# The order of the loads on one queue: an expert stage's weights against the memory weights and rows that follow them

## The chip, the cores and the metric

The kernel runs on one core of one Trainium2 chip. The metric is the time of one execution on the device in microseconds, as the median of several runs. All times in the rows are microseconds from the start of the profiled span, unless they are marked ns.

## What is computed

The reference is one hybrid transformer block (two attentions, then 32 experts of which each of 512 tokens uses two), followed by a second block of two layers, A and B, each of which also attends to 256 memory rows. All of it is float32. The change touches the experts and the step from them to layer A:

```python
for e in range(N_EXPERTS):                                   # 32, EXPERT_FF = 256
    hid = jax.nn.silu(jnp.matmul(h, w_gate[e])) * jnp.matmul(h, w_up[e])
    out = out + jnp.matmul(hid, w_down[e]) * combine[:, e:e + 1]
...
x = rmsnorm(x + m, final_norm_g)                             # the first block's end
...
kv = rms_norm(mem, mem_gain) @ w_kv                          # for layer A and for layer B
h = rms_norm(x, norm_gain[l])
cols = h @ w_in
```

## The kernel before

A matrix product in full precision is made from three products of split operands: each weight unit of 128 x 1024 floats (512 KB) is loaded raw, copied into a high part on ACT (line 229) and subtracted into a low part on DVE, every eighth on POOL (line 232). The experts' units are used raw, without a split.

All weights go through one object, `Stream` (line 196 on), in the order of one plan. `advance` emits loads (lines 214 and 217, all on SP's queue) in the plan's order as far as `ahead` allows, and stops at the first unit whose ring of tiles is full; `get` calls `advance` and hands out the next unit. A plan entry names its lane, that is, the ring that it is loaded into. The experts' 192 units are spread over seven lanes, so that tiles that are free in this stage serve as weight tiles: m (12 tiles), x (4), h (3), p and q (5 each: the high and low parts of the split weights), v (3: the raw weights), t (4). `_dealt` deals them out: the first 19 units are twelve m, four x and three h, then all lanes mix, and the last 32 units use m, x and h, the last 16 only m and h. The units of a pair of experts are 8 for gate and up and 4 for down; the first 8 units are pair 0's gate and up, then each step brings the next pair's 8 and this pair's 4. After the experts' units stand layer B's memory weights: four w_mv and four w_mk, in lane w.

The loop over the pairs (lines 1468 to 1493) is a block in which PE, ACT, DVE and POOL keep the order of the program: gate and up of the next pair (`gate_up`, line 1405), turning the tokens that `gather` fetched (`turn_tokens`, line 1390), the turned hidden row (`turned`, line 1418), and down (`down`, line 1431), whose result POOL scatters into `yd` (line 1436). SP isn't in that block: a scheduler places SP's instructions by its own estimate of when they can run, within what their tiles allow.

At j = 13 the loop emits the loads of the memory rows for layer B, two halves in tiles of ring m (`mem_load`, line 634), and reads the number of further rounds of experts into a register of each engine (line 1492). At j = 14 `ws.upto` lets the first two of w_mv be split. Behind the loop `mem_split` splits the memory halves, and `upto` lets all eight memory weights be split as far as tiles allow. Then the rows of x1, the residual, are loaded back (line 1501), and each engine reads a branch over the further rounds (an If, line 1549), which isn't taken here.

Behind the If, SP loads the row of gains gF (line 1077) and the experts' results from `yd` (lines 1563 and 1564), DVE adds them to x1's rows (lines 1566 and 1567), PE makes layer B's memory rows meanwhile (lines 370 to 372), turns x2 (line 404) and goes on with layer A. R (line 428), the rows' norms, needs the square of gF.

Of the kernel before, what the change touches and what calls it, by code (L numbers as in the profile page):

```python
# [16 lines left out]
AF = mybir.ActivationFunctionType  # L17
# [292 lines left out]
def build(tc, A, out, dbg=None):  # L310
    nc = tc.nc
    ctx = ExitStack()
    dbg = dbg or {}
    V, S, G, T = nc.vector, nc.scalar, nc.gpsimd, nc.tensor
# [8 lines left out]
    def acc():  # L323
        return ps.tile([128, 512], F32, name="acc", tag="acc", bufs=2)
# [191 lines left out]
    def pump(steps, n=None):  # L516

        if n != 0:
            for i, _ in enumerate(steps):
                if i + 1 == n:  # L520
                    return

    def xtile(name):
        return xp.tile([128, 1024], F32, name=name, tag="xn", bufs=4)
# [45 lines left out]
    ws = Stream(nc, [(ap, "w") for ap in plan1 + kv0] + moe_u + [(ap, "w") for ap in plan2], ahead=3)  # L570
# [58 lines left out]
    def mem_load(pool):  # L629

        res = []
        for j in range(2):
            res.append(pool.tile([128, 1024], F32, name="mem", tag="mraw", bufs=MR))
            nc.sync.dma_start(res[j], mTd[:, 1024 * j:1024 * j + 1024])
        return res

    def mem_split(pool, raw):
        res = []
        for t in raw:
            hi, lo = (pool.tile([128, 1024], F32R, name="mT", tag="mT", bufs=4) for _ in range(2))  # L640
            S.activation(hi, t, AF.Copy)
            V.tensor_tensor(lo, t, hi.bitcast(F32), OP.subtract)
            res += [(hi[:, q:q + 256], lo[:, q:q + 256]) for q in range(0, 1024, 256)]
        return res
# [429 lines left out]
    def bcast_row(pool, off, n, name, tag=None, bufs=1):  # L1074
        t = pool.tile([128, n], F32, name=name, tag=tag or name, bufs=bufs)
        r = A["rows"]
        nc.sync.dma_start(t, bass.AP(tensor=r.tensor, offset=r.offset + off, ap=[[0, 128], [1, n]]))
        return t
# [53 lines left out]
    x1v = x1d.rearrange("(c p) d -> c p d", p=128)  # L1132
# [57 lines left out]
    order = ExitStack()  # L1190
# [186 lines left out]
    def gather(j, ix):  # L1377

        nc.gpsimd.indirect_dma_start(out=xgs[j % 2], out_offset=None, in_=x1d,
                                     in_offset=bass.IndirectOffsetOnAxis(ap=ix, axis=0),  # L1380
                                     bounds_check=511, oob_is_err=False)

    def turn_tokens(j):

        xg = xgs[j % 2]
        res = []
        for q in range(2):
            tp = tpp()
            for k in range(4):
                T.transpose(tp[:, k * 128:k * 128 + 128], xg[:, (4 * q + k) * 128:(4 * q + k) * 128 + 128], ident)  # L1390
            t = hchunk("xgt")
            V.tensor_tensor(t.rearrange("p (k n) -> p k n", k=4), tp.rearrange("p (k n) -> p k n", k=4),  # L1392
                            vec(V_FFN + 4 * q, 4)[:, :, None].to_broadcast([128, 4, 128]), OP.mult)
            res += [t[:, k * 128:k * 128 + 128] for k in range(4)]
        return res
# [3 lines left out]
    def gate_up(get, X, p, us):  # L1399

        for u in us:
            w = [get(), get()]
            for k in range(2):
                for e, z in enumerate(sides):
                    T.matmul(p[z], X[2 * u + k][:, z], w[e][k], start=u + k == 0, stop=u + k == 4)  # L1405

    def hidden(p, hr, w):

        th = hchunk("th")[:, :256]
        S.activation(th, p[:, :256], AF.Tanh, scale=hr)  # L1410
        V.scalar_tensor_tensor(th, th, 1.0, p[:, :256], op0=OP.add, op1=OP.mult)
        V.scalar_tensor_tensor(th, th, w, p[:, 256:], op0=OP.mult, op1=OP.mult)
        return th

    def turned(th):
        tp = tpp()
        for k in range(2):
            T.transpose(tp[:, k * 128:k * 128 + 128], th[:, k * 128:k * 128 + 128], ident)  # L1418
        t = hchunk("hid")[:, :256]
        S.activation(t, tp[:, :256], AF.Copy)  # L1420
        return t

    def down(get, t, ox):

        y = big("y", "y", 2)
        for n in range(2):
            w = [get(), get()]
            p = scp()
            for k in range(2):
                for e, z in enumerate(sides):  # L1430
                    T.matmul(p[z], t[:, k * 128 + NS * e:k * 128 + NS * e + NS], w[e][k], start=k == 0, stop=k == 1)  # L1431
            if n:
                V.tensor_copy(y[:, 512:], p)  # L1433
            else:
                S.activation(y[:, :512], p, AF.Copy)
        nc.gpsimd.indirect_dma_start(out=yd, out_offset=bass.IndirectOffsetOnAxis(ap=ox, axis=0),
                                     in_=y, in_offset=None, bounds_check=1023, oob_is_err=False)
# [23 lines left out]

    order = ExitStack()
    ET = mybir.EngineType
    order.enter_context(tc.manual_schedule(engines={ET.PE, ET.Activation, ET.DVE, ET.Pool}))
    own = len(plan1) + 8 + 192
    ws.upto = own
    pg, Xnext = acc(), None
    for j in range(-1, 16):
        if j >= 0:
            th = hidden(pg, rw[:, j:j + 1], cw[:, j:j + 1])  # L1470
        if j < 15:
            Xg = Xnext or Xg
            pg = acc() if j >= 0 else pg
            gate_up(ws.get, Xg, pg, range(3))
        if j < 14:
            Xnext = turn_tokens(j + 2)
            if j < 12:
                gather(j + 4, idx[:, j + 4:j + 5])
        if j >= 0:
            t = turned(th)  # L1480
        if j < 15:
            gate_up(ws.get, Xg, pg, range(3, 4))
        if j >= 0:
            down(ws.get, t, odx[:, j:j + 1])
        if j == 0:
            pump(kv)
        if j == 13:
            mem2 = mem_load(mo)
        if j == 14:
            ws.upto = own + 2  # L1490
        if j == 13 and not dbg.get("noif"):
            nv = nc.values_load(next_i[0:1, 0:1], min_val=0, max_val=14)
    mT = mem_split(mo, mem2)
    ws.upto = own + 8
    ws.advance()
    order.close()
    vB_steps = memory_steps(ws, mT, store_v, (scp, otp))

    x2 = [xtile("x2") for _ in range(4)]
    for c in range(4):  # L1500
        nc.sync.dma_start(x2[c], x1v[c])


    def extra(e):
# [47 lines left out]
    gF = bcast_row(mo, 0, 1024, "gF", "mraw", MR)  # L1552
# [3 lines left out]
    ms = []  # L1556
    gF2 = big("gF2", "mraw", MR)
    with tc.manual_schedule(engines={ET.PE, ET.Activation, ET.DVE, ET.Pool}):
        S.activation(gF2, gF, AF.Square)
        kmB = [mo.tile([128, 512], F32, name="kmB", tag="mraw", bufs=MR) for _ in range(2)]  # L1560
        ms, ms2 = ([big("m", "mraw", MR) for c in range(4)] for _ in range(2))
        for c in range(4):
            nc.sync.dma_start(ms[c], yd[128 * c:128 * c + 128, :])
            nc.sync.dma_start(ms2[c], yd[512 + 128 * c:640 + 128 * c, :])
        def add_experts(c):
            V.tensor_tensor(x2[c], x2[c], ms[c], OP.add)
            V.tensor_tensor(x2[c], x2[c], ms2[c], OP.add)
            tap("x2", x2[c], c)

        def square(c):  # L1570
            S.activation(ms[c], x2[c], AF.Square, accum_out=s3[:, c:c + 1])
        pump(vB_steps, AFTER[0])
        add_experts(0)
        pump(vB_steps, AFTER[1])
        add_experts(1)
        square(0)
        pump(vB_steps)
        kv = mem_k(1, mT, mo, lambda j: kmB[j])
        tps = [bank() for bank in (scp, scp, scp, otp, tpp, tpp)]

        def beside(c):
            if c != 1:
                pump(kv, AFTER[c + 2])
            if c in (0, 2):
                add_experts(2 + c // 2)
            if c == 3:
                ws.upto = own + 10
                ws.advance()
        hT = transposed(x2, gFA, hp_, "h", 16, tps=tps, more=scp, before=beside)
        ws.upto = None  # L1590
        for c in range(1, 4):
            square(c)
        for c in range(4):
            V.tensor_tensor_reduce(ms2[c], ms[c], gF2, 1.0, 0.0, OP.mult, OP.add, s4[:, c:c + 1])

        V.tensor_scalar(a12[:, 1], s3, 1.0 / 1024, EPS, OP.mult, OP.add)
        V.tensor_scalar(a12[:, 0], s4, 1.0 / 1024, None, OP.mult)
        V.scalar_tensor_tensor(a12[:, 0], a12[:, 1], EPS, a12[:, 0], op0=OP.mult, op1=OP.add)
        G.tensor_tensor(r12, a12, mhalf.rearrange("p (a c) -> p a c", a=2), OP.pow)
        pump(kv, 2)  # L1600
# [493 lines left out]
```

## Time and profile before

| | us |
|---|---|
| median of 3 runs | 1861.84 |
| lowest and highest | 1859.59 and 1862.24 |
| the profiled execution | 1861.34 |
| its span | 1859.6 |
| PE busy | 1797.6 (97%) |
| DVE, ACT, POOL busy | 881.7, 731.5, 359.4 |
| queue of SP | 77184 packets, 248.43 MB |

The page of the profile gives busy times for the whole span and then in 40 slices of 46.5 us; the experts lie in slices 11 to 16. Busy shares of the span are a mean over stages with different limits, so the stage is to be read from views of its own stretch.

### The profile page before, as it was taken

How to read it: one execution, taken by the hardware profiler on the slowest of the kernel's cores; microseconds unless marked ns; L12 is line 12 of the kernel's file. 1: busy time of each engine (PE TensorE's matmuls, PEld its weight loads, DVE VectorE, ACT ScalarE, POOL GpSimd, SP SyncE). 2: the span in 40 equal slices, each digit the busy share in tenths (PEclk: the TensorE clock that was granted, in tenths of full speed). 3: DMA queues.
4: the chain of work that ended last, by engine and by line, in shares of the span. 5: the costliest groups of instructions: out<-in, count | busy, mean ns of one | idle time of the engine just before them, and what ended most of it. 6: DMA issues, size and time to landing. Idle time of an engine off the chain costs nothing.

```text
span 1859.6 us, 25386 instructions
## 1 busy us (share of the span) xinstructions
PE 1797.6 (97%) x9466; PEld 1386.2 (75%) x9466; DVE 881.7 (47%) x1864; ACT 731.5 (39%) x1747; POOL 359.4 (19%) x461
## 2 busy tenths in 40 slices
PE   8999999999899886999999999999999999999999
PEld 8857776788533322798989799989788787777887
DVE  4389765365422112842443422342575336667571
ACT  5475355343101002534554424454563333233450
POOL 1301200011211101114424104524200002212210
PEclk9999999999999998999999999999999999999999
DMA  5221222178999998532311122311242332211231
GB/s 180 79 69 35 74 69 74 57 247 302 354 413 410 405 407 333 223 127 91 104 56 53 62 91 91 100 59 46 69 135 93 114 106 65 68 58 58 69 113 57
DMA packets 82787, 261.14 MB, mean 140 GB/s; under 512 B 11872, under 2 KB 13792, under 8 KB 82656
## 3 DMA queue, kind: packets, MB, share of 16 engines
q1 hardware_dynamic: 77184, 248.43, 37.8%
q0 software_dynamic: 4608, 8.40, 1.2%
q10 hardware_dynamic: 864, 2.62, 0.3%
q8 instruction: 76, 1.25, 0.3%
q14 instruction: 55, 0.45, 0.1%
HBM read 248.92 MB, written 18.87 MB: 144 GB/s over the span
## 4 chain that ended last, share of the span: by engine, by line
PE 57%; DVE 2%; ACT 1%; POOL 0%; issue 0%; DMA 0%; ACTq 0%; POOLq 0%; DVEq 0%
PE acc L370 14%; PE acc L371 13%; PE acc L372 13%; PE sc L370 2%; PE sc L372 2%; PE sc L371 2%; PE sc L1964 1%; PE sc L1760 1%; PE tp L1701 1%; PE sc L1763 1%; PE tp L1768 1%; PE oT L1777 1%; PE oT L2012 1%; DVE wlo L232 1%; ACT whi L229 0%; PE oT L1772 0%
## 5 line engine op out<-in xcount | busy, mean ns | idle before, releaser
L370 PE MATMUL acc<-whi,hh 128*128 128x512 f32 (+2 forms) x936 | 382.1, 410 | 1.4 <-ACT hh L383 0.6
L371 PE MATMUL acc<-wlo,hh 128*128 128x512 f32 (+2 forms) x936 | 371.7, 398 | 0.0
L372 PE MATMUL acc<-whi,hl 128*128 128x512 f32 (+2 forms) x936 | 371.2, 399 | 0.0
L232 DVE TENSOR_TENSOR wlo<-wraw,whi 128x1024 fp32r<-128x1024 f32 (+4 forms) x213 | 249.2, 1176 | 228.8 <-ACT whi L229 228.1
L229 ACT ACTIVATE whi<-wraw 128x1024 fp32r<-128x1024 f32 (+4 forms) x243 | 243.2, 1003 | 263.1 <-PE acc L371 112.7
L370 PEld LDWEIGHTS acc<-whi,hh 128*128 128x128 f32 x936 | 222.9, 238 | 27.7 <-issue 2.8
L371 PEld LDWEIGHTS acc<-wlo,hh 128*128 128x128 f32 x936 | 223.5, 239 | 22.4 <-issue 1.7
L372 PEld LDWEIGHTS acc<-whi,hl 128*128 128x128 f32 x936 | 222.5, 238 | 21.6
L370 PE MATMUL acc<-hh,whi 128*128 128x512 f32 x448 | 184.8, 412 | 0.3 <-DVE rsa L364 0.3
L372 PE MATMUL acc<-hh,wlo 128*128 128x512 f32 x448 | 177.7, 397 | 0.0
L371 PE MATMUL acc<-hl,whi 128*128 128x512 f32 x448 | 176.8, 395 | 0.0
L232 POOL TENSOR_TENSOR wlo<-wraw,whi 128x1024 fp32r<-128x1024 f32 (+3 forms) x30 | 69.1, 2305 | 528.4 <-ACT whi L229 441.5
L365 POOL TENSOR_TENSOR rs<-rsa,mhalf 128x4 f32<-128x4 f32 (+1 forms) x80 | 79.4, 992 | 328.4 <-DVE rsa L362 270.1
L713 ACT ACTIVATE hjk<-acc 128x128 bf16<-128x128 f32 x232 | 64.3, 277 | 104.2 <-PE acc L372 73.3
L370 PEld LDWEIGHTS acc<-hh,whi 128*128 128x128 f32 x448 | 84.5, 189 | 21.9 <-issue 5.6
L1405 PE MATMUL acc<-mraw,xgt 128*64 128x512 f32 x232 | 97.4, 618 | 3.3 <-DMA mraw<-in_w_moe 3.2
L372 PEld LDWEIGHTS acc<-hh,wlo 128*128 128x128 f32 x448 | 84.2, 188 | 19.8 <-issue 1.0
L371 PEld LDWEIGHTS acc<-hl,whi 128*128 128x128 f32 x448 | 84.5, 189 | 15.5
L716 DVE TENSOR_TENSOR nat<-acc,rs 128x512 f32<-128x512 f32 x52 | 35.9, 691 | 61.4 <-POOL rs L365 43.5
L1420 ACT ACTIVATE hid<-tp 128x256 f32<-128x256 f32 x16 | 6.1, 384 | 149.5 <-PE tp L1418 149.5
L1433 DVE COPY y<-sc 128x512 f32<-128x512 f32 x16 | 11.1, 692 | 107.3 <-PE sc L1431 107.3
L1392 DVE TENSOR_TENSOR xgt<-tp,c_vecs 128x512 f32<-128x512 f32 x32 | 20.6, 686 | 84.5 <-PE tp L1390 80.3
(539 smaller groups left out, 3179.4 us busy)
## 6 DMA issues: line engine op xcount, KB each, us to landing
mraw<-in_w_moe SPq DMA_DIRECT2D x86, 512.0 KB, 10.0
wraw<-in_w_qka SPq DMA_DIRECT2D x48, 512.0 KB, 3.9
xraw<-in_w_moe SPq DMA_DIRECT2D x25, 512.0 KB, 9.7
wraw<-in_w_va SPq DMA_DIRECT2D x24, 512.0 KB, 4.3
hraw<-in_w_moe SPq DMA_DIRECT2D x44, 256.0 KB, 9.6
praw<-in_w_moe SPq DMA_DIRECT2D x22, 512.0 KB, 9.8
qraw<-in_w_moe SPq DMA_DIRECT2D x21, 512.0 KB, 9.6
wraw<-in_w_qfb SPq DMA_DIRECT2D x16, 512.0 KB, 3.5
```

Of the source, the lines that this page charges most:

```text
L229: nc.scalar.activation(hi, raw, AF.Copy)
L232: eng.tensor_tensor(lo, raw, hi.bitcast(F32), OP.subtract)
L365: G.tensor_tensor(r[:, :m], t[:, :m], mhalf[:, :m], OP.pow)
L370: T.matmul(p, a[0], b[0], start=start, stop=False)
L371: T.matmul(p, a[0], b[1], start=False, stop=False)
L372: T.matmul(p, a[1], b[0], start=False, stop=stop)
L713: S.activation(jk, p[:, h * 128:h * 128 + 128], AF.Square, accum_out=st[:, h:h + 1])
L716: V.tensor_tensor(t.rearrange("p (h d) -> p h d", h=nh), p.rearrange("p (h d) -> p h d", h=nh), r[:, :nh, None].to_broadcast([128, nh, 128 ...
L1392: V.tensor_tensor(t.rearrange("p (k n) -> p k n", k=4), tp.rearrange("p (k n) -> p k n", k=4), vec(V_FFN + 4 * q, 4)[:, :, None].to_broadc ...
L1405: T.matmul(p[z], X[2 * u + k][:, z], w[e][k], start=u + k == 0, stop=u + k == 4)
L1701: T.transpose(tp[:, c * 128:c * 128 + 128], nat[c][:, j * 128:j * 128 + 128], ident)
L1760: T.matmul(p[32 * j:32 * j + 32, :256], q0[:, 128 * j + c:128 * j + 128:4], k0[:, 128 * BASE[j]:128 * BASE[j] + 256], start=True, stop=True)
```

## The change

SP joins the engines that keep the program's order in the loop's block. The memory halves are loaded at j = 14 instead of 13, and x1's rows right behind them. In front of the If only two memory weights are split; the others, as far as tiles allow, are split behind it. The square of gF moves from ahead of that to behind the turning of x2.

```diff
-    order.enter_context(tc.manual_schedule(engines={ET.PE, ET.Activation, ET.DVE, ET.Pool}))
+    order.enter_context(tc.manual_schedule(engines={ET.PE, ET.Activation, ET.DVE, ET.Pool, ET.SP}))
...
-        if j == 13:
+        if j == 14:
             mem2 = mem_load(mo)
-        if j == 14:
-            ws.upto = own + 2
+            x2 = [xtile("x2") for _ in range(4)]
+            for c in range(4):
+                nc.sync.dma_start(x2[c], x1v[c])
         if j == 13 and not dbg.get("noif"):
             nv = nc.values_load(next_i[0:1, 0:1], min_val=0, max_val=14)
     mT = mem_split(mo, mem2)
-    ws.upto = own + 8
+    ws.upto = own + 2
     ws.advance()
     order.close()
     vB_steps = memory_steps(ws, mT, store_v, (scp, otp))
-
-    x2 = [xtile("x2") for _ in range(4)]
-    for c in range(4):
-        nc.sync.dma_start(x2[c], x1v[c])
...
     with tc.manual_schedule(engines={ET.PE, ET.Activation, ET.DVE, ET.Pool}):
-        S.activation(gF2, gF, AF.Square)
+        ws.upto = own + 8
+        ws.advance()
...
         hT = transposed(x2, gFA, hp_, "h", 16, tps=tps, more=scp, before=beside)
         ws.upto = None
+        S.activation(gF2, gF, AF.Square)
```

## Rows read from the trace of the kernel before

**Rows 1.** Stretches: length, busy PE, PEld, DVE, ACT, POOL, PEclk, DMA share, GB/s.
```profile
488.00:508.00 20.00, 19.65 (x102) 8.25 (x100) 5.61 (x10) 2.54 (x5) 3.24 (x4) 1.00 1.03 413
...
605.00:724.00 119.00, 97.50 (x376) 32.06 (x374) 17.11 (x31) 9.52 (x21) 10.10 (x10) 0.93 1.02 402
724.00:728.00 4.00, 2.22 (x12) 0.94 (x14) 2.07 (x4) 2.22 (x3) 0.97 (x1) 1.00 0.55 214
```

**Rows 2.** PE's timeline: start, length, what, idle before and its releaser.
```profile
737.36 0.77 PE L370 MATMUL sc<-whi,mT 128*128 128x512 f32 x1 [7.49 <-DVEq L1549]
```

**Rows 3.** Loads issued from 467 to 487: count, size, median us to landing.
```profile
praw<-in_w_moe SPq DMA_DIRECT2D x5, 512.0 KB, 7.5
qraw<-in_w_moe SPq DMA_DIRECT2D x5, 512.0 KB, 7.2
vraw<-in_w_moe SPq DMA_DIRECT2D x3, 512.0 KB, 6.0
traw<-in_w_moe SPq DMA_DIRECT2D x3, 512.0 KB, 6.9
```

**Rows 4.** SP's timeline: first issue of the group, its length, count.
```profile
487.64 13.96 SPq L217 DMA_DIRECT2D mraw<-in_w_moe  x12
```

**Rows 5.** PE's timeline in the first pairs of experts.
```profile
485.68 0.64 PE L1405 MATMUL acc<-mraw,xgt 128*64 128x512 f32 x1
...
497.30 1.89 PE L1405 MATMUL acc<-xraw,xgt 128*64 128x512 f32 x8
...
502.69 2.31 PE L1431 MATMUL sc<-hraw,hid 128*64 128x512 f32 x9
```

**Rows 6.** Loads issued from 660 to 727 that aren't experts' weights.
```profile
x<-x1d SPq DMA_DIRECT2D x4, 512.0 KB, 8.7
wraw<-in_w_mv SPq DMA_DIRECT2D x3, 512.0 KB, 8.8
mem<-mTd SPq DMA_DIRECT2D x2, 512.0 KB, 9.1
```

**Rows 7.** A load issued from 728 to 735, with few others in flight.
```profile
wraw<-in_w_mv SPq DMA_DIRECT2D x1, 512.0 KB, 4.7
```

**Rows 8.** SP's queue from 468 to 508: packets, MB, share of 16 engines.
```profile
q1 hardware_dynamic: 3779, 13.78, 89.0%
```

**Rows 9.** The page's groups of splits: count, busy, mean ns, idle before.
```profile
L229 ACT ACTIVATE whi<-wraw 128x1024 fp32r<-128x1024 f32 (+4 forms) x243 | 243.2, 1003 | 263.1 <-PE acc L371 112.7
L232 POOL TENSOR_TENSOR wlo<-wraw,whi 128x1024 fp32r<-128x1024 f32 (+3 forms) x30 | 69.1, 2305 | 528.4 <-ACT whi L229 441.5
```

**Rows 10.** DVE's timeline before the If and at the sums.
```profile
730.55 2.35 DVE L642 TENSOR_TENSOR mT<-mem,mT 128x1024 fp32r<-128x1024 f32 x2
...
734.25 1.23 DVE L232 TENSOR_TENSOR wlo<-wraw,whi 128x1024 fp32r<-128x1024 f32 x1 [0.21 <-ACT whi L229]
...
749.89 1.23 DVE L1567 TENSOR_TENSOR x<-x,m 128x1024 f32<-128x1024 f32 x1
```

**Rows 11.** Line 1549, the If: ns min/median/max, first and last start.
```profile
L1549 SPq EVENT_SEMAPHORE  x9: 17/17/17, 734.2 to 734.8; - x9
...
L1549 SPq COMPARE_BRANCH  x1: 50/50/50, 729.9 to 729.9; - x1
...
L1549 DVEq COMPARE_BRANCH  x1: 72/72/72, 734.3 to 734.3; - x1
...
L1549 DVEq EVENT_SEMAPHORE  x1: 21/21/21, 737.2 to 737.2; - x1
```

**Rows 12.** SP's timeline behind the If, the first of the experts' rows.
```profile
738.42 0.33 SPq L1563 DMA_DIRECT2D m<-yd  x1
```

**Rows 13.** PE's timeline, turning the second tile of x2.
```profile
754.48 0.49 PE L404 MATMUL sc<-c_ident,x 128*128 128x128 f32 x3
```

**Rows 14.** DVE's and PE's timelines: R is copied, and PE reads it.
```profile
778.57 0.17 DVE L428 COPY R<-r 128x4 f32<-128x4 f32 x1 [1.71 <-POOL r L1599]
...
784.21 1.05 PE L432 MATMUL tp<-c_ident,R 128*128 128x128 f32 x8
```

## The prediction

> **What bounds the kernel now.** The page first: PE is busy 97% of the span, but its slices from the twelfth on dip while the DMA line stands at 9. So the second view is the table of stretches over the experts [rows 1]: between 488 and 724 us the 16 DMA engines are full (share 1.02 to 1.03, 402 and 413 GB/s) and PE is not (97.5 of 119 us after 605). In that stage a 512 KB unit of weights costs 0.524 MB / 0.41 MB per us = 1.28 us of queue, and whatever leaves the queue empty, or puts other bytes ahead of the last expert's, moves the end. After 728 PE is the bound again, so a shift of PE's start on the memory rows of layer B (737.36, ended by DVE's step over the If, line 1549 [rows 2]) runs through to the end of the kernel.
>
> Third view, the queue's issues. Which order do they have against the program? The plan (`_dealt`) is mmmmmmmmmmmm xxxx hhh m p q x m t h v m p ... . `advance` stops at the first unit whose ring is full. Twelve m fill their ring, so unit 19, the thirteenth m, is emitted only in the second `get`, and all p, q, v and t after it. Counting the rings by hand: 19 to 21 are emitted at get 1, 22 to 24 at get 13 (x needs unit 12's tile), 25 to 37 at get 17 (h needs unit 16's). In the trace it is different: 5 p, 5 q, 3 v and 3 t, sixteen units, are issued between 467 and 487 [rows 3], ahead of the first further m at 487.64 [rows 4], which waits for PE's first expert matmuls of 485.68 [rows 5]. So today's scheduler, with SP free, lifts sixteen loads out of the experts' loop over a blocked one, into a time in which the queue has nothing else. At the other end it does the opposite: three w_mv, four x1 rows and two memory transfers [rows 6], nine units, stand among the last experts' weights.
>
> **The change part by part.** SP joins the engines that keep the program's order. Both liftings go.
>
> 1. *The start, a loss.* With SP in program order m at 487.64 is the queue's head, and p and q stand behind it. Unit 22 waits for units 12 and 13, whose matmuls end at 497.30 + 1.89 = 499.2; unit 25 waits for units 16 and 17, whose matmuls run in the nine of 502.69, to about 504.5 [rows 5]. By 508 the queue can therefore have moved units 19 to 24 and, after a landing of 4.7 us in an empty queue [rows 7], about one more: 7. Before moved 13.78 MB on this queue by then [rows 8], 26.3 units. The lag is 19.3 units x 1.28 = 24.7 us. Bounds: 9 units moved by 508 (no latency after 504.5) give 22.1, 6 give 26.0. I take 7 because the 4.7 us are a measured landing. Nothing gives the lag back: the engines are full in the old kernel from 488 on, so the new one can only be as full.
>
> 2. *The end, a gain.* The queue of before runs dry at about 725.5: the share over 724 to 728 is 0.55, 2.2 us of work [rows 1]. With the nine units behind the weights, the last expert's unit lands 9 x 1.28 = 11.5 us earlier in the order: 725.5 + 24.7 - 11.5 = 738.7. Three w_mv and two memory transfers follow (6.4): 745.1. The four x1 rows follow until 750.2; they are first read by the sums of line 1566, over 15 us later, price nothing.
>
> 3. *The If.* In front of it DVE now has the two memory halves and two weight splits instead of four. ACT's copy takes 1.0 [rows 9], DVE 1.2 each [rows 10]: second half 745.1 + 1.0 + 1.2 = 747.3, first split until 748.5; the second starts there and the branch is read behind it, as before at 734.3, beside the split of 734.25. DVE came out 2.9 later (737.2) [rows 11], and PE began 0.15 after that. So 748.5 + 2.9 + 0.2 = 751.6 where it was 737.36: **+14.3**. The three splits put behind the If are on ACT, DVE and POOL; PE has the 24 matmuls of the first two units before it reads the third: nothing. If DVE's 2.9 were as short as a plain step, the sum falls by up to 2.9.
>
> 4. *The experts' rows, read back.* SP issues one load behind each split, so it reads its branch behind the second (749.7) and is out 4.3 later [rows 11]. The last w_mk waits for POOL's split: landing 749.7 + 4.7, ACT 1.0, POOL 2.3 = 757.7 [rows 7, 9]; the first m row behind it at 758.1, where it was 738.42 [rows 12]: 19.7 later, against 14.3 for PE. The second tile's sum ends at 749.89 + 1.23 + 19.7 = 770.8 [rows 10]; PE wants it at 754.48 + 14.3 = 768.8 [rows 13]: **+2.0**. The others have more slack. Bounds: 0, if the free scheduler behind the If puts the m rows ahead of the w_mk, and 5.4, if no slack helps.
>
> 5. *Small ones.* SP's register load (line 1492) now stands in the queue at j = 13, below 1 us while the loads ahead of it are still moving: nothing. The square of gF goes from ahead of ACT's splits to behind the turning of x2: 1.0 us on ACT, covered because R is ready at 778.57 and PE reads it only at 784.21 [rows 14]; without that cover 1.0.
>
> Sum: 14.3 + 2.0 = 16.3 on the profiled execution's 1861.34 us (its span 1859.6 and 1.7 around it; the median of the three runs is 1861.84): **1877.6 us**.
>
> The rate of 1.28 us is the row's. The Trainium skill ("DMA: Bandwidth & Descriptors", section "Where 436 GB/s comes from") says that for transfers from HBM to SBUF the HBM side, some 358 GB/s, binds. By that rule a unit would cost 1.46 us and the sum would be about 1880.4; the 402 and 413 GB/s of this trace [rows 1] speak against it, and the row decides.
>
> The Trainium skill ("DMA: Bandwidth & Descriptors", section "Anatomy of one DMA — SWDGE (gpsimd) path") says that DMA engines don't wait on semaphores, the issuing sequencer does, before dispatch. By that rule a load whose tile is still read holds back every load behind it, as step 1 has it; the trace agrees as far as the m of 487.64 starts when PE's first expert matmuls end, but no run here shows ready loads held behind it.
>
> **Rivals.** *Faster:* the sixteen loads still go out early, be it that the order is kept only loosely or that the change doesn't hold them. Then step 1 is gone and the rest stays: 1877.6 - 24.7 = 1852.9. For it: everything at the end is sound, nine units out of the weights' way. Against it: PE, ACT, DVE and POOL are in the same kind of block already, and their instructions of the loop stand in program order in the trace. It decides from a lag of 8.4 us on, 6.6 units: fewer held back, and the change is a gain. Chance 0.14. *About the same:* only half of the sixteen are held: 1877.6 - 12.3 = 1865.3; chance 0.06. *Slower still:* the strict order stops the queue again. By the plan a load is emitted 31 units ahead in the middle but only 14 near the end, and the landing of 8.7 to 9.1 us [rows 6] keeps some 7 in flight; a PE that lags 6 units behind the data would empty the queue. Three such stops of 2.9, one for each of the last pairs: 1886. Against it: PE has nothing else to wait for there and reads a unit when it lands. Chance 0.08.
>
> **How the numbers follow.** My case holds 0.72, from 1877.6 - 2.6 (lag) - 2.0 (rows) - 2.0 (part of DVE's step) = 1871 to 1877.6 + 1.3 + 3.4 = 1882. To leave out no more than 2 in 10 the range takes in the third rival and the edge of the second: 1866 to 1886. A measurement of this kernel can tell about 0.2% (3.7 us) from no change; faster by more 0.14, within it 0.06, slower by more 0.80.
>
> **What would show it.** The issues of p, q, v, t none before 487; the DMA share near zero from about 462 to 487 and low until 505; PE waiting on loads in each pair from about 515 on, not only near the end; the last expert's h issued near 730 with no w, x1 or memory transfer ahead of it; two weight splits, not four, before DVE's branch, and PE's start near 751. The prediction is wrong if the sixteen are still ahead of 487, if the queue is not full after 508, or if PE's start and the end shift by different amounts.

## The result and the profile after

| | before | after |
|---|---|---|
| median of four runs each, same chip | 1860.7 us | 1886.6 us |
| profiled execution, its span | 1861.3, 1859.6 us | 1885.7, 1883.9 us |
| queue traffic, 468 to 508 us | 13.78 MB | 4.28 MB |
| end of the last expert matmul | 729.9 | 742.2 |
| PE's first matmul behind the If | 737.4 | 755.1 |
| first vm copy on ACT | 750.5 | 776.1 |

The changed kernel is slower: 1.014 times the time before, 95% interval 1.0122 to 1.0157. The profiled executions lie 24.3 us apart. The forecast was 1877.6, with a range up to 1886; the direction was right, and the loss was half as large again. The vm of the table is the tile into which ACT copies layer B's memory values out of the accumulators (banks) that PE wrote them to; PE can write to such a bank again only behind that copy.

The stretches at the start (columns: length, busy time of PE, PEld, DVE, ACT, POOL with counts, granted clock, DMA share, GB/s), then SP's queue over both of them (packets, MB, share):

```profile
468.00:488.00 20.00, 17.25 (x99) 12.60 (x99) 13.32 (x63) 4.46 (x20) 6.97 (x7) 0.91 0.14 37
488.00:508.00 20.00, 19.65 (x102) 8.22 (x100) 5.23 (x9) 2.91 (x6) 3.53 (x4) 1.00 0.67 239
```

```profile
q1 hardware_dynamic: 1314, 4.28, 29.1%
```

SP's timeline there (start, length, queue, line, what):

```profile
487.27 0.33 SPq L217 DMA_DIRECT2D mraw<-in_w_moe  x1
487.64 0.43 SPq L217 DMA_DIRECT2D praw<-in_w_moe  x1
488.11 0.43 SPq L217 DMA_DIRECT2D qraw<-in_w_moe  x1
498.83 0.33 SPq L217 DMA_DIRECT2D xraw<-in_w_moe  x1
```

The m that waits for PE's first expert matmul is now the head, p and q stand behind it, and the next x stops the queue again for 10.7 us. [rows 3] and [rows 8] are what stood here before. From 508 on the queue is as full as in [rows 1]. The other end, on SP, ACT, DVE and PE:

```profile
730.09 1.66 SPq L214 DMA_DIRECT2D hraw<-in_w_moe  x2
732.05 2.28 SPq L217 DMA_DIRECT2D wraw<-in_w_mv  x3
735.31 1.58 SPq L634 DMA_DIRECT2D mem<-mTd  x2
737.79 2.81 SPq L1491 DMA_DIRECT2D x<-x1d  x4
750.08 0.33 SPq L217 DMA_DIRECT2D wraw<-in_w_mv  x1
751.22 0.33 SPq L217 DMA_DIRECT2D wraw<-in_w_mk  x1
```

```profile
746.61 1.06 ACT L641 ACTIVATE mT<-mem 128x1024 fp32r<-128x1024 f32 x1 [0.20 <-DMA mem<-mTd]
...
748.84 3.49 DVE L232 TENSOR_TENSOR wlo<-wraw,whi 128x1024 fp32r<-128x1024 f32 x3
...
755.13 0.77 PE L370 MATMUL sc<-whi,mT 128*128 128x512 f32 x1 [12.98 <-DVEq L1546]
```

All nine transfers stand behind the last h. PE's last expert matmul ends at 742.2, but mem's second half lands at 746.6, and PE idles 13.0 us where [rows 2] had 7.5. Then a second stop, which the forecast did not have. SP, ACT and PE behind the If, then the stretch of the stop and the one behind it (columns as above, the granted clock ahead of the DMA share):

```profile
757.58 0.37 SPq L217 DMA_DIRECT2D wraw<-in_w_mk  x1
758.05 0.37 SPq L1562 DMA_DIRECT2D m<-yd  x1
...
761.37 0.33 SPq L217 DMA_DIRECT2D wraw<-in_w_mk  x1
...
765.14 0.33 SPq L217 DMA_DIRECT2D wraw<-in_w_mk  x1
```

```profile
771.40 1.06 ACT L229 ACTIVATE whi<-wraw 128x1024 fp32r<-128x1024 f32 x1 [6.58 <-DMA wraw<-in_w_mk]
...
775.16 1.06 ACT L229 ACTIVATE whi<-wraw 128x1024 fp32r<-128x1024 f32 x1 [1.66 <-DMA wraw<-in_w_mk]
776.12 0.58 ACT L1457 ACTIVATE vm<-sc 128x512 f32<-128x512 f32 x1
...
776.76 0.48 PE L404 MATMUL sc<-c_ident,x 128*128 128x128 f32 x1 [4.38 <-ACT vm L1457]
```

```profile
772.00:776.70 4.70, 0.37 (x3) 0.14 (x1) 4.04 (x4) 3.04 (x6) 0.00 (x0) 0.80 1.01 394
776.70:782.00 5.30, 5.23 (x18) 4.35 (x19) 5.23 (x5) 2.38 (x4) 0.00 (x0) 0.53 0.62 201
```

In the kernel before, SP and ACT had here:

```profile
735.34 2.85 SPq L217 DMA_DIRECT2D wraw<-in_w_mk  x3
```

```profile
750.51 0.60 ACT L1457 ACTIVATE vm<-sc 128x512 f32<-128x512 f32 x1 [0.79 <-PE sc L372]
```

There three w_mk loads stood ahead of the first m row [rows 12]. In the changed kernel the last three w_mk loads go out among the eight m rows; the ones issued at 761.37 and 765.14 are read at 771.40 and 775.16, 10 us later. ACT stands on them, the vm copies stand behind ACT's splits, and PE waits 4.38 us for a bank that vm empties. After that stop PE works at a granted clock of 0.53, the lower of its two levels (1.2 of 2.4 GHz) for nearly all of that stretch, although it is busy 5.23 of 5.30 us.

### The profile page after: what moved, and what is told of

The parts are those of the page before. It is cut to its first block, busy times and chain, and to the rows that moved or that the text cites. A ratio compares the mean times of both kernels' runs of the same rounds, so it can differ in the third digit from the quotient of the medians.

```text
span 1883.9 us, 25354 instructions
## 1 busy us (share of the span) xinstructions
PE 1818.8 (97%) x9466; PEld 1393.5 (74%) x9466; DVE 881.6 (47%) x1864; ACT 731.8 (39%) x1747; POOL 359.3 (19%) x461
## 4 chain that ended last, share of the span: by engine, by line
PE 55%; DVE 2%; DMA 1%; ACT 1%; issue 0%; POOL 0%; SPq 0%; ACTq 0%; POOLq 0%; DVEq 0%
PE acc L370 14%; PE acc L371 13%; PE acc L372 13%; PE sc L370 2%; PE sc L372 2%; PE sc L371 2%; PE sc L1963 1%; PE sc L1759 1%; PE tp L1700 1%; PE sc L1762 1%; PE tp L1767 1%; PE oT L1776 1%; PE oT L2011 1%; ACT whi L229 1%; DMA wraw<-in_w_mk 1%; DVE wlo L232 1%
## 5 line engine op out<-in xcount | busy, mean ns | idle before, releaser
L371 PEld LDWEIGHTS acc<-wlo,hh 128*128 128x128 f32 x936 | 223.8, 239 | 22.1 <-issue 1.7
L1433 DVE COPY y<-sc 128x512 f32<-128x512 f32 x16 | 11.1, 692 | 113.6 <-PE sc L1431 113.6
## 6 DMA issues: line engine op xcount, KB each, us to landing
qraw<-in_w_moe SPq DMA_DIRECT2D x21, 512.0 KB, 10.2
```

Source lines behind the costliest of these rows:

```text
L371: T.matmul(p, a[0], b[1], start=False, stop=False)
```

## Experiments on the start

Two accounts were open. Theory: the loss at the start is the sixteen lifted loads. Rival: the strict order as such stops the queue through the whole loop. Four kernels take the change apart. Of each kernel one execution was traced, and the stage's start moves between the traces: PE's first expert matmul stands at 485.68 before, at 485.30 in the changed kernel, and between 484.97 and 488.00 in the others. A place at a fixed time carries that shift.

**The sixteen by hand.** Edit to the changed kernel, ahead of the expert block (`early` issues the named units and hands the tiles to `advance` later):

```
+    lanes = [n for _, n in ws.plan]
+    ws.early(sorted(i for n, k in (("p", 5), ("q", 5), ("v", 3), ("t", 3))
+                    for i in [i for i, z in enumerate(lanes) if z == n][:k]))
```

> The changed kernel, with SP kept in the program's order, but the sixteen p, q, v and t units are issued by hand ahead of the expert block, where the scheduler of the kernel before had put them. Theory 1 (the lag is those sixteen units and nothing else): between 468 and 508 us the queue moves about 13.8 MB again instead of 4.28 MB, which is 18 units x 1.28 us = 23 us; the tail of the changed kernel stays as it is, so 1886.6 - 23 = about 1863, between 1860 and 1866. Rival (the strict order stops the queue again and again in the expert loop, whatever stands at its start): little comes back, 1878 to 1887, with stretches under a DMA share of 0.9 between 520 and 700 us.

Measured: 1869.0 us, 1.0039 times before (1.0024 to 1.0053), above the 1860 to 1866 expected. That is 17.6 us below the changed kernel, not 23; counted against the kernel before, each on its own chip, the loss falls from 25.9 to 6.7 us. The stretches:

```profile
468.00:488.00 20.00, 17.25 (x111) 13.05 (x111) 12.99 (x59) 2.97 (x12) 5.84 (x5) 0.91 0.72 273
488.00:508.00 20.00, 19.65 (x98) 8.14 (x94) 5.81 (x15) 3.15 (x13) 4.11 (x4) 1.00 0.83 320
```

By 508 the queue has moved 10.63 MB, against 13.78 and 4.28. So both theories hold in part: the sixteen are most of it, but even with them early the strict order keeps later loads behind a blocked x, which goes out at 501.08, 11.6 us behind the m ahead of it (0.83 in the second stretch). The queue is 3.15 MB or 6.0 units behind, 7.7 us; 1.9 us of that are this trace's later start (487.55), which leaves some 5.8 for the order. From 508 to 720 the share is 1.03, so the stops through the whole loop, which the rival expected, are not there. PE's last expert matmul ends at 727.2.

**SP free until the last steps.** Edit to the changed kernel:

```
-    order.enter_context(tc.manual_schedule(engines={ET.PE, ET.Activation, ET.DVE, ET.Pool, ET.SP}))
+    order.enter_context(tc.manual_schedule(engines={ET.PE, ET.Activation, ET.DVE, ET.Pool}))
...
     for j in range(-1, 16):
+        if j == 13:
+            order.close()
+            order = ExitStack()
+            order.enter_context(tc.manual_schedule(engines={ET.PE, ET.Activation, ET.DVE, ET.Pool, ET.SP}))
```

> The changed kernel, but SP joins the engines in the program's order only from the last two experts' steps on (j == 13); until then its loads are in the scheduler's order, as before. The tail is that of the changed kernel. Theory 1: as the run with the sixteen units put ahead by hand, about 1863 (1860 to 1866). Rival (strict order is what stops the queue in the loop): this one comes back to 1863 and the other does not. If both come back alike, the order inside the loop costs nothing and the start is the whole loss. In both the three weight rows, two rows of mem and four rows of x1 stand behind the last expert's weights, so PE's last expert matmul should be earlier than before by up to 9 units x 1.28 = 11.5 us, and the If step should then begin by mem's landing, not by the matmuls.

Measured: 1867.7 us, ratio 1.003 (1.0019 to 1.0041), again above the 1860 to 1866 expected. It moves 12.82 MB by 508 (its first expert matmul stands at 487.09), and the last h goes out 7.9 us earlier than before. PE, and ACT behind it:

```profile
735.30 0.76 PE L370 MATMUL sc<-whi,mT 128*128 128x512 f32 x1 [12.89 <-DVEq L1550]
```

```profile
753.56 1.06 ACT L229 ACTIVATE whi<-wraw 128x1024 fp32r<-128x1024 f32 x1 [6.58 <-DMA wraw<-in_w_mk]
```

The experts end 7.5 us earlier than before (722.4), PE behind the If starts only 2.1 us earlier, and the median is 5.5 us above that of before on the same chip (1862.2). The changed kernel's two stops stand there again, 12.89 us at the If and 6.58 us on w_mk. The end of the change, which the forecast counted as a gain, loses by itself.

**The strict order alone**, on the kernel before:

```
-    order.enter_context(tc.manual_schedule(engines={ET.PE, ET.Activation, ET.DVE, ET.Pool}))
+    order.enter_context(tc.manual_schedule(engines={ET.PE, ET.Activation, ET.DVE, ET.Pool, ET.SP}))
```

> The kernel before with one edit alone: SP is added to the engines in the program's order. Everything else (w_mv and w_mk asked for in the program ahead of the If, mem a step earlier, x1's rows at the block's end, gF2's square ahead) is as before. Theory 1: the sixteen units are late again, +23 us at the start; w_mv, mem and x1's rows go where the program of before has them, so part of the 11.5 us is not given back; the w_mk loads stand ahead of the If and ahead of the m rows, so ACT does not stand on them afterwards. Sum 1861 + 23 - 5 to 0 = 1879 to 1884. Rival (the other edits, not the strict order, make the loss): 1861 to 1866.

Measured: 1886.4 us, ratio 1.0135 (1.0116 to 1.0154), the time of the whole change, and above the 1879 to 1884 expected. One edit reproduces the loss, yet by another way. It moves 3.93 MB by 508; x1's and mem's transfers keep their places among the weights and only w_mv goes behind them, so less is gained at the end: the last h goes out at 737.29 and PE starts at 762.29, both 7 us later than in the changed kernel. But behind the If nothing is lost:

```profile
762.29 0.77 PE L370 MATMUL sc<-whi,mT 128*128 128x512 f32 x1 [10.77 <-DVEq L1549]
...
776.13 0.58 ACT L1457 ACTIVATE vm<-sc 128x512 f32<-128x512 f32 x1
```

vm comes 13.8 us behind PE's start; it is 13.1 in the kernel before and 21.0 in the changed one. So the tail's loss is not the strict order's.

**Everything but the strict order.**

```
-    order.enter_context(tc.manual_schedule(engines={ET.PE, ET.Activation, ET.DVE, ET.Pool, ET.SP}))
+    order.enter_context(tc.manual_schedule(engines={ET.PE, ET.Activation, ET.DVE, ET.Pool}))
```

> The changed kernel without SP among the engines in the program's order: only the rest of the edits (w_mv and w_mk asked for later, mem and x1's rows one step later in the program, gF2's square moved) against the kernel before. Theory 1: the start is that of before, no loss; the scheduler lifts w_mv, mem and x1's rows in among the experts' weights as it did before; the w_mk loads go behind the If among the m rows, and ACT stands on them for some us: 1861 + 0 to 6 = 1861 to 1867. Rival (the later edits carry a good part of the 25 us): 1872 or more.

Measured: 1870.9 us, ratio 1.0045 (1.0031 to 1.006), between the theory's 1861 to 1867 and the rival's 1872; the profiled execution took 1867.9. PE starts within 0.6 us of before (737.97), and vm is 7.0 us later:

```profile
754.53 1.06 ACT L229 ACTIVATE whi<-wraw 128x1024 fp32r<-128x1024 f32 x1 [6.53 <-DMA wraw<-in_w_mk]
```

The other edits thus cost 6 to 9 us by themselves, nearly all of it behind the If: PE stops for 4.25 us on vm, which stands behind that w_mk split, and later twice on DVE at line 412 (1.02 and 1.60 us).

## Experiments on the tail

Theory A: the w_mk loads are late because they are queued among the m rows. Theory B: their raw buffers (three for all w loads) come free late, since the change moved two splits of w_mv behind mem's.

**The order alone.** Edit to the changed kernel, the block behind the If:

```
-    with tc.manual_schedule(engines={ET.PE, ET.Activation, ET.DVE, ET.Pool}):
+    with tc.manual_schedule(engines={ET.PE, ET.Activation, ET.DVE, ET.Pool, ET.SP}):
```

> The changed kernel with SP kept in the program's order behind the If as well: the last three w_mk loads go ahead of the eight m rows instead of among them. Start and everything up to the If as in the changed kernel. Theory A (ACT stands on w_mk because these loads are queued among the m rows; their buffers are free by 758): the vm copies, at 776.1 in the changed kernel, 21.0 us behind PE's start behind the If, come about 13.5 us behind it, as in the kernel before; the m rows leave 3 to 4 us later, which gives back up to 2: 1886.6 - 5 to 7 = about 1880 (1878 to 1882). Rival B (the loads are late because their raw buffers come free late, the splits of w_mv having been moved behind mem's): the queue only waits in another place, vm stays 19 to 21 us behind PE's start: 1884 to 1888.

Measured: 1882.9 us, ratio 1.0119 (1.0104 to 1.0134), 3.7 us below the changed kernel. SP and ACT:

```profile
757.00 2.63 SPq L217 DMA_DIRECT2D wraw<-in_w_mk  x3
759.86 0.33 SPq L1561 DMA_DIRECT2D m<-yd  x1
```

```profile
763.63 1.06 ACT L229 ACTIVATE whi<-wraw 128x1024 fp32r<-128x1024 f32 x1 [0.19 <-DMA wraw<-in_w_mk]
769.76 1.05 ACT L229 ACTIVATE whi<-wraw 128x1024 fp32r<-128x1024 f32 x1
770.71 0.58 ACT L1457 ACTIVATE vm<-sc 128x512 f32<-128x512 f32 x1
```

The buffers were free: three loads leave in 2.6 us. vm comes 5.4 us earlier than in the changed kernel and PE's 4.38 us stop is gone. That is theory A, with a smaller yield than the 5 to 7 expected. What is left behind PE's start is two waits on DVE for the low parts of the next operand, where the kernel before has one, of 1.02 us:

```profile
782.50 0.66 PE L412 MATMUL sc<-c_ident,x 128*128 128x128 f32 x4 [1.02 <-DVE hl L384]
784.58 1.12 PE L412 MATMUL sc<-c_ident,x 128*128 128x128 f32 x4 [1.42 <-DVE hl L384]
```

**The splits back ahead of mem's.** Edit to the changed kernel (`own` is the first w_mv's place in the plan):

```
         if j == 14:
+            ws.upto = own + 2
             mem2 = mem_load(mo)
...
+    ws.advance()
     mT = mem_split(mo, mem2)
-    ws.upto = own + 2
+    ws.upto = own + 8
```

> The changed kernel with one part of it undone: two splits of w_mv stand ahead of mem's split again (ws.upto = own + 2 at j == 14, ws.advance() ahead of mem's split, own + 8 behind it), so raw buffers come free ahead of the branch and three of the four w_mk loads leave ahead of it. The start is as in the changed kernel. Theory B (the raw buffers' late release makes the tail's loss): vm comes 13 to 14 us behind PE's start instead of 21.0; PE starts up to 1.5 us later, since DVE waits for the fourth w_mv ahead of the branch: 1886.6 - 6 = about 1880 (1878 to 1883). Theory A (only the order against the m rows counts) expects the same here, since these loads also get ahead of the m rows; the two are told apart by the run with the order alone changed. Rival C (the wait is the clock's or the expert rows' and not w_mk's): 1885 to 1888.

Measured: 1885.9 us, ratio 1.0131 (1.0116 to 1.0146), the changed kernel's time, where 1878 to 1883 was expected. vm comes 14.8 us behind PE's start, so the tail is mended as in the run before. But the fourth w_mv now has to be split ahead of the branch, and it lands late:

```profile
755.36 1.06 ACT L229 ACTIVATE whi<-wraw 128x1024 fp32r<-128x1024 f32 x1 [4.93 <-DMA wraw<-in_w_mv]
...
759.59 0.77 PE L370 MATMUL sc<-whi,mT 128*128 128x512 f32 x1 [15.53 <-DVEq L1548]
```

PE starts 4.5 us later (759.59 against 755.13). Idle time and clock behind PE's start cost 7.2 us instead of 11.1, so the later start uses up all of the gain. Of the 4.5 us, 1.9 are not shown to be the edit's: the experts end that much later in this trace, whose first expert matmul stands at 487.39. B's edit mends the tail too, since it also puts w_mk ahead of the m rows; that the order alone does nearly as much (vm 15.7 us behind PE's start) says that the buffers are not needed to explain it.

## Experiments on the end's gain

Is there a version in which the gain reaches the end? The start and the tail were undone together.

> Both losses undone: SP joins the engines in the program's order only from j == 13 on (the sixteen units are early again), and two splits of w_mv stand ahead of mem's split. What is left of the change is the end: w_mv, mem and x1's rows behind the last expert's weights. The run with the first edit alone had PE's first matmul behind the If at 735.3 (before 737.4) and the vm copies at 758.3 (before 750.5). Theory: vm about 13.5 us behind PE's start, at 749 to 750.5, so 1867.7 - 8 = about 1860, level with the kernel before to 3 us below it (1857 to 1862): the end's gain of up to 11.5 us on the experts is used up by the If's own chain (mem, split, branch), and only 0 to 2 us reach the end. Rival (the end's gain comes through once nothing else is late): 1850 to 1855.

> As the run with both losses undone, and mem's two rows issued one step earlier (at j == 13, as in the kernel before), ahead of the last expert's weights. Theory (what bounds PE's start behind the If is the chain mem, split, branch): mem lands some 5 us earlier and the last expert's weights 2 x 1.3 us later; PE's start moves earlier by 0 to 2.5 us, to 733 to 735, the time 1857 to 1860. Rival (the fourth w_mv, whose load waits for the first split, bounds the branch): no change against the run without this edit, within 1 us.

The edits are those shown above (SP free until j == 13, the splits back), in the second run with `mem2 = mem_load(mo)` at j == 13. Measured: 1867.8 us, ratio 1.0036 (1.0024 to 1.0048), and 1866.1 us, ratio 1.0031 (1.002 to 1.0042); the theories' 1857 to 1862 held in neither. The experts end 6 to 7 us earlier than before, PE starts at 737.8 and 736.1, and behind it DVE waits for the m rows in both:

```profile
749.02 1.23 DVE L1571 TENSOR_TENSOR x<-x,m 128x1024 f32<-128x1024 f32 x1 [5.05 <-DMA m<-yd]
```

In both runs the fourth w_mv is what ACT waits for last ahead of the branch, 5.41 us in the first and 3.00 in the second, as the second run's rival had it; with mem early PE's start still moved by 1.7 us, more than the rival's 1.

**x1's rows alone.** On the kernel before, only the four x1 rows moved; the w_mv loads issued by hand at j == 12, SP strict from j == 14 (first run) or j == 13 (second):

```
+        if j == 12:
+            ws.early(range(own, own + 3))
+        if j == 14:
+            order.close()
+            order = ExitStack()
+            order.enter_context(tc.manual_schedule(engines={ET.PE, ET.Activation, ET.DVE, ET.Pool, ET.SP}))
...
         if j == 14:
+            x2 = [xtile("x2") for _ in range(4)]
+            for c in range(4):
+                nc.sync.dma_start(x2[c], x1v[c])
             ws.upto = own + 2
```

> The kernel before, with one piece of the change's end alone: only x1's four rows go behind the last expert's weights. The three w_mv loads are issued by hand at j == 12, so that they stay among the earlier experts' weights; mem stays at j == 13, the splits and gF2's square stay as in the kernel before; SP is held to the program's order only from j == 14 to the branch, which is what keeps x1's rows from being lifted. Theory (four units of 1.28 us leave the full queue, and fit into the hole between the last expert's weights and the branch; the chain mem, split, branch is moved along with the experts): PE's last expert matmul 5.1 us earlier, at 724.8, PE's start behind the If at 732 to 733, nothing lost behind it: 1860.6 - 4 to 5 = about 1856 (1855 to 1858). Rival (the fourth w_mv and the w_mk loads, now behind x1's rows, bound the branch and the tail): 1859 to 1863.

> The same with SP in the program's order from j == 13 on, so that mem's two rows also stand one step later and three w_mk loads instead of two stand ahead of the branch. Theory: as the run from j == 14, or up to 2 us slower, because mem lands later and SP reaches the branch later: 1856 to 1859. If the split of the queue at the branch matters (SP waits for a raw buffer ahead of the branch and the expert rows go out later), 1859 to 1862.

Measured: 1861.6 us, ratio 1.0 (0.9991 to 1.0009), and 1864.8 us, ratio 1.002 (1.0011 to 1.0029). The expected 4 to 5 us did not come, and the second is above its rival's 1862 too. In the first run's trace the experts end 1.8 us earlier, not 5.1. But this trace starts late (first expert matmul at 487.53) and has moved 12.50 MB by 508, not 13.78, which is 3.1 us of queue; 1.8 and 3.1 are 4.9, so the four units did leave the experts' way. What takes the gain is the rival's wait: ACT stands on the fourth w_mv, which lands behind the x1 rows, 7.9 us after its issue at 726.26 ([rows 7] had 4.7), and PE idles 10.93 us at the If instead of 7.49.

```profile
734.20 1.06 ACT L241 ACTIVATE whi<-wraw 128x1024 fp32r<-128x1024 f32 x1 [4.62 <-DMA wraw<-in_w_mv]
735.53 1.06 ACT L241 ACTIVATE whi<-wraw 128x1024 fp32r<-128x1024 f32 x1 [0.28 <-DMA wraw<-in_w_mk]
```

**x1's rows behind the If.** The same, with the four loads asked for behind `ws.upto = own + 8` and its `ws.advance()`:

> As the run with x1's four rows alone moved (SP in the program's order from j == 14), but asked for behind the splits, so that they leave behind the If, after the last w_mk load and ahead of the expert rows; the fourth w_mv is no longer queued behind them. Theory (in that run the fourth w_mv, landing 7.9 us after its issue behind x1's rows, held DVE 3.0 us ahead of the branch and used up the gain): the fourth w_mv lands in under 5.5 us again, DVE does not wait for it, PE starts 7.5 us behind the last expert matmul, at 735 to 736 instead of 739.1; the expert rows leave about 5 us later relative to PE's start, into a slack of about as much ahead of the first transposes: 1861.6 - 3 = 1857 to 1860. Rival (that slack is too small): PE then waits for the added rows instead, 1860 to 1864.

Measured: 1865.4 us, ratio 1.0019 (1.001 to 1.0028). The first half held: PE starts at 733.20, 4.2 us earlier than before. The second went to the rival, at a higher price than expected. DVE and PE:

```profile
749.07 1.23 DVE L1584 TENSOR_TENSOR x<-x,m 128x1024 f32<-128x1024 f32 x1 [6.39 <-DMA m<-yd]
```

```profile
751.79 0.66 PE L416 MATMUL sc<-c_ident,x 128*128 128x128 f32 x2 [2.06 <-DVE x L1585]
...
754.31 0.48 PE L416 MATMUL sc<-c_ident,x 128*128 128x128 f32 x1 [1.86 <-ACT vm L1469]
```

DVE stands on the first m row, ACT's square of that sum waits 9.0 us for DVE, and the next w_mk split and vm stand behind the square in ACT's order. So the tail has no slack for four more units. Nothing run here beats the kernel before. In that kernel the queue is full from 742 to 755, right behind the hole at 724 to 737:

```profile
724.00:730.00 6.00, 4.09 (x18) 1.36 (x18) 3.63 (x6) 4.00 (x6) 0.97 (x1) 1.00 0.48 167
730.00:737.00 7.00, 0.00 (x0) 0.00 (x0) 5.26 (x5) 3.82 (x4) 2.74 (x2) 0.66 0.67 235
737.00:742.00 5.00, 4.64 (x11) 3.71 (x12) 0.00 (x0) 1.06 (x1) 0.83 (x1) 0.50 0.95 338
742.00:755.00 13.00, 13.00 (x61) 10.60 (x61) 10.93 (x10) 5.42 (x7) 0.00 (x0) 0.98 1.02 414
```

The transfers that were moved off the experts' weights are read within 25 us of the last expert, by a chain (mem, splits, branch, w_mk, m rows) that needs the queue itself.

## Why the prediction was right and wrong

**Step 1, the start: right, 1.5 us too dear.** None of the sixteen was issued ahead of 487. The queue moved 8.2 units by 508, not 7: the lag is (13.78 - 4.28) / 0.524 = 18.1 units, 23.2 us, within the bounds of 22.1 to 26.0. One of its waits was wrong: unit 25, an h, was to stand until 504.5 for PE's matmuls on unit 16, and it went out at 500.21, right behind unit 24 and ahead of those matmuls (502.32), since its tile was free. That no lag is given back held: the queue is full from 508 on. The Trainium skill's rule ("DMA: Bandwidth & Descriptors", section "Anatomy of one DMA — SWDGE (gpsimd) path") that the issuing sequencer waits, not the DMA engine, agrees with this trace for ready loads too: p and q left 0.4 and 0.8 us behind the m that held them.

**Step 2, the end's gain: right on the queue.** The last h of the kernel before, on SP, is

```profile
718.25 1.56 SPq L214 DMA_DIRECT2D hraw<-in_w_moe  x2
```

and 730.09 in the changed kernel, 715.24 with the sixteen by hand, 710.40 with SP strict only from j == 13. Less the lag of each by 508 (23.2, 7.7 and 2.3 us), it left 11.4, 10.7 and 10.2 us earlier; the forecast was 11.5. Steps 1 and 2 together put the experts' end 12.3 us later; the forecast's 24.7 - 11.5 was 13.2.

**Step 3, the If: its chain right, 3.5 us too cheap.** PE started 17.8 us later, not 14.3. Mem's second half landed at 746.6, not 745.1 (1.5). That is more than it looks: the last h moved 11.8 us and not 13.2, so the queue in front of mem was 1.4 us ahead of the forecast, and the landing behind it 2.9 us later than a count of units at 1.28 us gives. The forecast took mem as landed when its turn on the queue was over; the two halves landed 10.0 us after their issues. DVE read its branch at 750.5, not 748.5, which is 0.5 more than mem's landing explains. And three splits, not two, stood ahead of the branch, although `ws.upto` was own + 2 there: DVE reads the branch at 750.5, when ACT's third copy ends, so the scheduler moves work across the If. DVE came out 4.5 us after reading the branch, not 2.9 (1.6), which the last section comes back to:

```profile
L1546 DVEq COMPARE_BRANCH  x1: 72/72/72, 750.5 to 750.5; - x1
L1546 DVEq EVENT_SEMAPHORE  x1: 21/21/21, 755.0 to 755.0; - x1
```

**Step 4, the rows read back: the step that failed.** It assumed the w_mk loads ahead of the m rows and priced the m rows' delay at 2.0; it took the other order as its lower bound, 0. The scheduler chose the other order, and that is the dear one: the m rows were in time, but the w_mk loads among them landed 10 us after issue, ACT's in-order splits stood on them, and the vm copies that empty PE's banks stand behind those splits. The end moved 24.3 where PE's start moved 17.8, so the step measured 6.5, above its upper bound of 5.4. (That the two shift by different amounts was one of the forecast's own signs of being wrong, although its sum had them 2.0 apart.) Summed over the 90 stretches of 1 us behind PE's start, idle time and the share of busy time lost to a lower granted clock are 3.6 us before and 11.1 after: idle went from 1.0 to 5.6, the clock's part from 2.6 to 5.5, together 7.5 us more, where the ends give 6.5. The forecast had no term for the clock, and its 2.9 are more than the step's whole 2.0. The error was to follow the m rows to their reader, and not the loads that the m rows displace to theirs. The order alone, set right, gives 3.7 us back; the rest, 2.8 us behind PE's start, goes with PE's two waits on DVE at line 412 and the clock behind them, and no single edit was found for it, so that its cause stays open.

**The miss.** 24.3 - 16.3 = 8.0: 3.5 in step 3 and 4.5 in step 4. The errors of steps 1 and 2 are inside step 3's 3.5, since mem stands behind the experts' weights on the queue and its landing starts the If: they made the queue too late by 1.4, and the landing took that back and more.

**The rivals.** "Faster" supposed that the sixteen stay early with the end sound, 1852.9. The run with SP free until j == 13 is that case, and gave 1867.7: its premise, that everything at the end is sound, was wrong, since the forecast gave the end by itself a net gain of 8.4 us, and in that run it is a loss of 5.5, of which some 2.3 are a start somewhat behind that of before in its trace. "About the same" is settled by the issues: none of the sixteen was early. "Slower still" by three more stops in the loop did not occur (the share from 508 to 742 is 1.01 to 1.03 throughout), but in the run with the sixteen by hand the strict order itself costs some 5.8 us near the start.

## What to carry to other kernels

On a queue that issues in order, price a moved load by what stands behind it, on the queue and then on the in-order engine that reads it, down to whoever waits for that engine's next instruction. Bytes taken from ahead of a full stage are a gain only if they aren't needed in the next few units of queue time after it; here nine units worth 11.5 us of queue gave nothing, since the following chain needed the same queue. And before an issue order is made strict, look for loads that the scheduler has lifted over a blocked one: the strict order alone cost as much as the whole change.

## What the hardware showed beyond expectation

- **The step over the If has two lengths on DVE.** From reading the branch to the event behind it took 2.9 us in the kernel before and 4.5 in the changed one. Over the thirteen kernels it was 2.9 to 3.0 in seven (the kernel before, the changed kernel with the splits back, both runs with the start and the tail undone, and the three that move only x1's rows) and 4.2 to 4.6 in six (the changed kernel, the four of the first experiments, the order alone). The traces part along the queues. In the 2.2 us behind the reading of the branch the seven have two or three packets on q14, which the profile calls instruction, and all queues together move 0.05 to 0.36 MB; the six have no such packet there, and 0.47 to 0.65 MB move. So the long step goes with data on the queues and a later q14 packet; that the one causes the other was not tested.
- **A stop of PE can cost clock behind it.** Behind the 4.38 us stop PE ran at a granted clock of 0.50 until about 781.5, some 2.5 us of work lost. In the kernel before, the one such stop behind the If, 1.02 us, had a granted clock of 1.00 behind it. The length of the stops alone does not decide: the two stops of 1.02 and 1.42 us at line 412 had 0.50 behind them in the run with the order alone (785 to 787), and 1.00 in the kernel with only the strict order (792 to 798).
- **A load's landing goes by what was issued ahead of it.** The same 512 KB took 4.7 us in a nearly empty queue [rows 7], 7.9 behind four x1 rows, and 10 among the m rows.
